# Rotary product of q and k: partner rows added by transfers of GpSimd's queue instead of by VectorE

## The chip, the core and the metric

The kernel runs on one core of one Trainium2 chip. The metric is the device time of one execution in microseconds. The core has a matrix engine (TensorE, PE in the profile, with its weight loads as PEld), a vector engine (VectorE, DVE), a scalar engine (ScalarE, ACT), GpSimd (POOL) and a queue-issuing engine (SyncE, SP). Each engine works through its own list of instructions in order; semaphores make one wait for another. Transfers (DMA) are issued by SP, ACT or POOL and then run beside the engines; those from POOL are the page's queue q0, those from SP its queue q1.

## The reference, cut to what matters

A decoder block on 512 tokens of width 1024, all in 32-bit floats:

```
h = rmsnorm(x);  [q | k | v | u_pool | u_gate] = h @ w_in
q, k: 8 heads x 2 components x 64 dims; the first 16 dims of each component are rotated:
    t1, t2 = t[..., :8], t[..., 8:16]
    t[..., :16] = [t1*cos - t2*sin, t2*cos + t1*sin]          # the other 48 dims stay
per head and block of 128 queries: p = softmax(q @ k^T, causal) for both components
    w = p[0] - lam * p[1];  o = w @ v;  rmsnorm over the 128 value dims
pooled branch from u_pool (windows 2, 4, 8, 16);  merged = sigmoid(gA)*o + sigmoid(gP)*pool
x = x + merged @ w_out
x = x + relu(rmsnorm(x) @ w_up)^2 @ w_down;  final rmsnorm
```

The scores q @ k^T do not change when the 64 dims of q and of k are put in another order, as long as both have the same one.

## The kernel before, in words

**Precision.** Each product of two float32 matrices is made of three passes of TensorE: both operands are split into a rounded high part and a low remainder (`wh_*`, `wl_*` for weights, `xh`, `xl` for activations, `gab`, `gss` for the MLP's input, `z` for its hidden layer). For weights, ACT casts the high part (L112, L120) and either DVE subtracts (L113), or ACT writes the negated high part (L121) and POOL's queue adds the weight to it by an accumulating transfer from memory (L122, 512 KB each).

**Stages.** First v for all tokens and q of head 0; from about 60 us the attention stage; from about 290 us the output projection with `w_out` (`po0_t` and `po1_t`: the two halves of the columns for the four blocks t of 128 tokens, L581 to L583); from about 350 us the MLP, to the end.

**Attention stage.** For head h, `qk(h)` projects 128 columns of q, then of k (24 matmuls of 128x512 each, L131, L132, L135; the result has 128 rows, two components of 64 dims, and 512 columns, the tokens). `rope` (L347 to L354) rotates it. The products with the tables: `q1 = acc*cosR` (L349); `sw` is a copy of acc with rows 0 to 7 and 8 to 15 of each 32 exchanged (stream_shuffle, L351); `sw = sw*sinR` (L352); `q1 = q1+sw` (L353). All four run on DVE, 128x512 each. The tables hold 1 and 0 in the rows that are not rotated; sinR holds the minus sign. The rotated q goes to `qs` (ACT casts, L375; DVE remainders, L376), the rotated k to `kz` (ACT, L379) and `ks` (ACT, L381; DVE, L382). `attn(h)` makes the scores `s` (L394, L395), the softmax (DVE L396, ACT L400), transposes the weights (`t`, L409), and multiplies with v (`o`, L417). Its result is squared and summed over rows (`sqo`, `sql` on POOL, L426, L427, on DVE for head 7; `ss` on PE, L429, L430). Between heads the list `fillers` puts 20 projections for the pooled branch and the gates (u, ga, gp); they are independent of the heads. `merge(h)` joins branches and makes `mh`, `ml`, which `w_out` needs.

**From attention to the MLP.** When `po0_t` and `po1_t` are complete, DVE adds them to x (L587), ACT squares and sums (L561), a row factor is made (ACT L571 to L573, DVE L574, L575), DVE makes `h2` of block t (L623), and PE transposes it into `h2Tt_0` and `h2Tt_1` (L629). For t = 0, 1, ACT casts these into the high part of `gab` (L641) and DVE subtracts the low part (L642); for t = 2, 3 they go through `hw`. The first products of the MLP, `um10` and `um20`, multiply the high part with the weight's high part at L759 and the low part at L761. They take 256 tokens at a time, so they need blocks 0 and 1 of `gab`.

**What sets the order.** The program is written with tiles; the framework turns it into one list for each engine at build time (`schedule_with_timeline_sim=True`, L989): it takes the operations by their place in the program and by its own estimate of when their inputs are there. Nothing is reordered when the program runs. So an edit of one step can move others on every engine. Waits come from buffers too: `q1` and `sw` have two buffers each.

Of the kernel before, what the change touches and what calls it, by code (L numbers as in the profile page):

```python
# [15 lines left out]
ALU = mybir.AluOpType  # L16
AX = mybir.AxisListType

P = 128
S = 512  # L20
D = 1024
# [21 lines left out]
    return out  # L43


SWAP = list(range(8, 16)) + list(range(0, 8)) + list(range(16, 32))

LAG = (2, 5, 7, 10, 12, 14, 15, 20)

# [2 lines left out]
def block_kernel(ctx, tc, xT, x_tok, gains, pos, consts, w_in, w_v, w_pool, w_out, w_up, w_dn, out):  # L52
    nc = tc.nc
    V, A, G, T = nc.vector, nc.scalar, nc.gpsimd, nc.tensor
# [17 lines left out]
    def bank(i, name):  # L72
        return ps.tile([P, S], F32, tag=f"b{i}", name=name)
# [13 lines left out]
    def tmp(tag, name, shape=(P, S), dt=F32, bufs=2):  # L87
        return tp.tile(list(shape), dt, tag=tag, name=name, bufs=bufs)
# [53 lines left out]
    for i in range(2):  # L142
# [19 lines left out]
    mask = cf.tile([P, S], F32, name="mask")  # L162
    G.memset(mask, 0.0)
    G.affine_select(
        out=mask[:, 384:512], in_=mask[:, 384:512], pattern=[[-1, P]],
# [51 lines left out]
    for n in range(2):  # L217
        accs = [bank((0, 1, 2, 3, 4, 5, 6, 0)[4 * n + t], f"v{n}_{t}") for t in range(NT)]
        for kk in range(4):
# [24 lines left out]
            if n == 0 and 0 < kk < 3:  # L244
                i = kk - 1
# [14 lines left out]
        for t in range(NT):  # L260
# [4 lines left out]
                out=vd[2], in0=av, scalar=rcol[:, t, 0:1], in1=vd[1],  # L265
                op0=ALU.mult, op1=ALU.subtract,
# [25 lines left out]
        out=r_, in0=posf.rearrange("p (t o) -> p t o", o=1).to_broadcast(sh),  # L292
        in1=invc.rearrange("p (o f) -> p o f", o=1).to_broadcast(sh), op=ALU.mult,
# [20 lines left out]
    arg = cf.tile([P, 2, NT, 8], F32, name="arg")  # L314
# [10 lines left out]
    for i, fill in ((0, 1.0), (1, 0.0)):  # L325
        tk = tmp("q1", f"rt{i}", (P, NT, 2, 8, 8))
        G.memset(tk, fill)
        for c in range(2):
            for x_ in range(2):
                sc = -1.0 if (i == 1 and x_ == 0) else 1.0  # L330
                V.tensor_scalar(out=tk[:, :, c, x_, :], in0=arg[:, i], scalar1=sc, scalar2=None, op0=ALU.mult)
        pt = bank((3, 2)[i], f"pt{i}")
        for t in range(NT):
            T.transpose(out=pt[:, t * P : t * P + P], in_=tk[:, t].rearrange("p c x f -> p (c x f)"), identity=ident)
        tab = cf.tile([P, S], F32, name=f"tab{i}")
        V.tensor_tensor(out=tab, in0=pt, in1=rb, op=ALU.mult)
        tabs.append(tab)
    cosR, sinR = tabs
# [8 lines left out]
    def rope(acc_, name):  # L347
        q1 = tmp("q1", f"q1{name}")
        V.tensor_tensor(out=q1, in0=acc_, in1=cosR, op=ALU.mult)  # L349
        sw = tmp("sw", f"sw{name}")  # L350
        V.stream_shuffle(out=sw, in_=acc_, mask=SWAP)  # L351
        V.tensor_tensor(out=sw, in0=sw, in1=sinR, op=ALU.mult)  # L352
        V.tensor_tensor(out=q1, in0=q1, in1=sw, op=ALU.add)  # L353
        return q1  # L354

    def proj(m, name, eng=None):
# [12 lines left out]
    def qk(h):  # L369
        qs = tp.tile([P, 2, S], F32R, tag="qs", name=f"qs{h}", bufs=2)  # L370
        ks = tp.tile([P, 2, S], F32R, tag="ks", name=f"ks{h}", bufs=2)
        kz = kzs[h % 2]
        q = rope(proj(h, f"q{h}", V) if h else q0, f"q{h}")
        for c, own, oth in ((0, lo_, hi_), (1, hi_, lo_)):
            A.copy(out=qs[own, c, :], in_=q[own])  # L375
            V.tensor_tensor(out=qs[oth, c, :], in0=q[own], in1=f(qs)[own, c, :], op=ALU.subtract)  # L376
        k = rope(proj(8 + h, f"k{h}", V), f"k{h}")
        for c, own, oth in ((0, lo_, hi_), (1, hi_, lo_)):
            A.copy(out=kz[own, c, :], in_=k[own])  # L379
        for c, own, oth in ((0, lo_, hi_), (1, hi_, lo_)):  # L380
            A.copy(out=ks[oth, c, :], in_=f(kz)[own, c, :])  # L381
            V.tensor_tensor(out=ks[own, c, :], in0=k[own], in1=f(kz)[own, c, :], op=ALU.subtract)  # L382
        return qs, ks, kz
# [609 lines left out]
```

## Time and profile before

| what | value |
|---|---|
| three runs | 677.84, 676.32, 676.32 us (median 676.32) |
| span of the profiled execution, first to last instruction | 675.2 us |
| the profiled execution's own time | not given on the page; its span lies 1.1 us under the median |
| granted TensorE clock, mean | 0.998 |
| PE busy | 665.3 us of the span (99%) |
| DVE busy | 529.1 us (78%) |
| ACT busy | 462.5 us (68%) |
| POOL busy | 123.0 us (18%), 137 instructions |
| moved by DMA | 109.34 MB, mean 162 GB/s |

The page gives busy time by engine, the same in 40 slices, the queues, the chain of work that ended last, the costliest groups of instructions and the transfers by line. Beside it stand answers about single stretches (windows), groups by line and form, and instructions in order of time. In a row of a group, the two numbers behind the bar are its busy time in us and the mean of one in ns, then the idle time of the engine just before and what ended it. A matmul of 128x512 is shown with some 390 ns, but matmuls overlap: what counts for the rate is the distance of their starts.

### The profile page before, as it was taken

Reading aid. Unit: us, or ns where it says so; the run is one execution under the profiler, and the core shown is the slowest. Engines: PE = TensorE matmul, PEld = TensorE weight load, DVE = VectorE, ACT = ScalarE, POOL = GpSimd, SP = SyncE. Lnnn points to the kernel's source line nnn. Section 1 sums busy time; section 2 is a strip of 40 time slices with the busy share of each in tenths; the row PEclk is TensorE's granted clock in tenths of the full one; section 3 lists DMA queues with packets and bytes.
Section 4 is the critical chain, followed back from the end, with each engine's and each line's share of the span. In section 5 each row is a group of like instructions: output and inputs, shape, how many; then the busy total and the mean of one; then the engine's idle time right before and its main releaser. Section 6 shows DMA issues by size and latency. Waiting matters only on the chain.

```text
span 675.2 us, 9995 instructions
## 1 busy us (share of the span) xinstructions
PE 665.3 (99%) x3686; PEld 579.9 (86%) x3686; DVE 529.1 (78%) x879; ACT 462.5 (68%) x741; POOL 123.0 (18%) x137
## 2 busy tenths in 40 slices
PE   9999999999999999999999999999999999999995
PEld 7788888888888888888889988899889998899884
DVE  6955877799979986975478989667994599747995
ACT  8465587978887698883477975367753696356874
POOL 6201110132133212520201020202103021210120
PEclk9999999999999999999999999999999999999999
DMA  8526574435254364574964678676969579493863
GB/s 272 189 71 182 126 152 125 102 94 126 87 139 105 101 171 94 126 193 177 309 194 79 196 172 241 153 179 155 234 190 197 200 156 260 125 213 131 213 125 124
DMA packets 32880, 109.34 MB, mean 162 GB/s; under 512 B 4032, under 2 KB 4928, under 8 KB 32832
## 3 DMA queue, kind: packets, MB, share of 16 engines
q0 software_dynamic: 10656, 38.80, 32.4%
q1 hardware_dynamic: 21744, 69.38, 29.0%
q8 instruction: 29, 0.48, 0.3%
q10 hardware_dynamic: 432, 0.52, 0.2%
q14 instruction: 19, 0.16, 0.1%
HBM read 106.59 MB, written 2.10 MB: 161 GB/s over the span
## 4 chain that ended last, share of the span: by engine, by line
PE 86%; DMA 5%; issue 5%; DVE 1%; ACT 1%; SPq 0%; DVEq 0%; POOLq 0%
PE dm L838 7%; PE dm L840 7%; PE dm L841 7%; PE um L759 7%; PE um L764 7%; PE um L761 7%; DMA wga_uNone<-w_up 5%; PE o L417 2%; PE ga L132 2%; PE ga L131 2%; PE gp L135 2%; PE k L132 2%; PE gp L132 2%; PE gp L131 2%; PE k L131 2%
## 5 line engine op out<-in xcount | busy, mean ns | idle before, releaser
L840 PE MATMUL dm<-wh_dt,z 128*128 128x512 f32 (+1 forms) x128 | 49.5, 387 | 0.0
L841 PE MATMUL dm<-wl_dt,z 128*128 128x512 f32 (+1 forms) x128 | 49.4, 386 | 0.0
L838 PE MATMUL dm<-wh_dt,z 128*128 128x512 f32 (+1 forms) x128 | 49.0, 387 | 0.0
L759 PE MATMUL um<-gss,wh_ut 128*128 128x256 f32 x192 | 48.1, 284 | 0.1
L761 PE MATMUL um<-gss,wh_ut 128*128 128x256 f32 x192 | 48.1, 283 | 0.0
L400 ACT ACTIVATE p<-p,st 128x128 f32<-128x128 f32 (+3 forms) x64 | 35.8, 560 | 14.1 <-DVE st L396 13.8
L112 ACT CAST wh_ut<-wga_uNone 128x1024 fp32r<-128x1024 f32 x24 | 24.9, 1053 | 28.8 <-PE dm L840 19.2
L856 DVE TENSOR_TENSOR x<-x,dm 128x512 f32<-128x512 f32 x48 | 32.8, 687 | 14.1 <-PE dm L841 14.0
L670 POOL DMA_DIRECT2D wga_dNone<-w_dn x16 | 14.2, 887 | 151.8 <-DVE wl_dt L113 151.8
L113 DVE TENSOR_TENSOR wl_ut<-wga_uNone,wh_ut 128x1024 fp32r<-128x1024 f32 x24 | 29.0, 1224 | 12.5 <-ACT wh_ut L112 12.5
L112 ACT CAST wh_ub<-wr_u 128x1024 fp32r<-128x1024 f32 x24 | 25.1, 1051 | 19.0 <-PE um L761 10.1
L670 POOL DMA_DIRECT2D wga_uNone<-w_up x18 | 15.6, 867 | 120.9 <-DVE wl_ut L113 86.9
L840 PE MATMUL dm<-wh_db,z 128*128 128x512 f32 x96 | 37.2, 389 | 0.0
L841 PE MATMUL dm<-wl_db,z 128*128 128x512 f32 x96 | 37.2, 389 | 0.0
L759 PEld LDWEIGHTS um<-gss,wh_ut 128*128 128x128 f32 x192 | 36.8, 192 | 0.3 <-ACT rawz L776 0.3
L761 PEld LDWEIGHTS um<-gss,wh_ut 128*128 128x128 f32 x192 | 36.9, 192 | 0.0
L838 PE MATMUL dm<-wh_db,z 128*128 128x512 f32 x96 | 35.8, 390 | 0.0
L113 DVE TENSOR_TENSOR wl_ub<-wr_u,wh_ub 128x1024 fp32r<-128x1024 f32 x24 | 29.2, 1222 | 7.9 <-ACT wh_ub L112 7.9
L112 ACT CAST wh_dt<-wga_dNone 128x1024 fp32r<-128x1024 f32 x24 | 24.8, 1050 | 14.6 <-issue 4.1
L735 DVE TENSOR_TENSOR z<-rawz,z 128x1024 fp32r<-128x1024 f32 x28 | 33.7, 1225 | 0.9 <-ACT z L732 0.9
L396 DVE CUSTOM_DVE_ANT_0 p<-s,mask 128x128 f32<-128x128 f32 (+3 forms) x64 | 30.3, 485 | 3.4 <-PE s L395 3.3
L732 ACT CAST z<-rawz 128x1024 fp32r<-128x1024 f32 x28 | 28.7, 1048 | 6.0 <-DVE rawz L741 4.9
(324 smaller groups left out, 2222.9 us busy)
## 6 DMA issues: line engine op xcount, KB each, us to landing
wr_u<-w_up SPq DMA_DIRECT2D x24, 512.0 KB, 5.3
wr_d<-w_dn SPq DMA_DIRECT2D x24, 512.0 KB, 4.2
wga_uNone<-w_up POOLq DMA_DIRECT2D x18, 512.0 KB, 6.7
wga_dNone<-w_dn POOLq DMA_DIRECT2D x16, 512.0 KB, 5.8
wr_k<-w_in SPq DMA_DIRECT2D x8, 512.0 KB, 3.3
wr_ga<-w_in SPq DMA_DIRECT2D x8, 512.0 KB, 3.3
wr_gp<-w_in SPq DMA_DIRECT2D x8, 512.0 KB, 4.2
wl_ga<-w_in POOLq DMA_DIRECT2D x8, 512.0 KB, 5.5
```

The source lines that it names most:

```text
L112: ins = A.copy(out=hi[:, sl], in_=raw[:, sl])
L113: (eng or G).tensor_tensor(out=lo[:, sl], in0=raw[:, sl], in1=f(hi)[:, sl], op=ALU.subtract)
L131: T.matmul(acc, lhsT=hi[:, c], rhs=rh[:, k, :], start=k == 0, stop=False)
L132: T.matmul(acc, lhsT=hi[:, c], rhs=rl[k], start=False, stop=False)
L400: A.activation(out=pr[:, c, :N], in_=pr[:, c, :N], func=AF.Exp, scale=-1.0, bias=st[:, c : c + 1], accum_out=st[:, 2 + c : 3 + c])
L735: V.tensor_tensor(out=z[:, 1], in0=r, in1=f(z[:, 0]), op=ALU.subtract)
L759: m = T.matmul(a_, lhsT=hi[:, c], rhs=rh[:, k, :], start=p + k == 0 and onto is None, stop=False, skip_group_check=True)
L761: T.matmul(a_, lhsT=hi[:, c], rhs=rl[:, k, :], start=False, stop=False, skip_group_check=True)
L764: m = T.matmul(a_, lhsT=lo[:, c], rhs=rh[:, k, :], start=False, stop=k == 3, skip_group_check=True)
L838: m = T.matmul(a_, lhsT=zh, rhs=hi[:, sl], start=p == 0 and start, stop=False, skip_group_check=True)
L840: T.matmul(a_, lhsT=zl, rhs=hi[:, sl], start=False, stop=False, skip_group_check=True)
L841: end = T.matmul(a_, lhsT=zh, rhs=lo[:, sl], start=False, stop=p == 3, skip_group_check=True)
```

## The change

The columns of q and k in `w_in` are put in another order on the host (once, outside the kernel): in each component of 64, the dims t1 stand at places 0, 8, ..., 56 and their partners t2 at places 4, 12, ..., 60; the other dims fill the places left. The tables are filled to match, with the minus sign at the t2 places of sinR. In `rope`, the shuffle (L351) and the sum (L353) go. DVE makes `q1 = acc*cosR` and `sw = acc*sinR`, both from acc. Then two accumulating transfers of POOL's queue add 16 rows of `sw` to 16 rows of `q1` each (rows 4, 12, ... to rows 0, 8, ... and the other way round; 16 rows of 2 KB, 32 KB). In the changed kernel the product from acc and sinR is L351 and the two transfers are L353; the line numbers of what runs on the chip are the same in both.

```diff
-SWAP = list(range(8, 16)) + list(range(0, 8)) + list(range(16, 32))
+ORDER = [p // 8 + 2 * (p % 8) if p % 4 == 0 else 16 + 6 * (p // 8) + p % 8 - 1 - p % 8 // 4 for p in range(64)]
...
-                sc = -1.0 if (i == 1 and x_ == 0) else 1.0
-                V.tensor_scalar(out=tk[:, :, c, x_, :], in0=arg[:, i], scalar1=sc, scalar2=None, op0=ALU.mult)
+                sc = -1.0 if (i == 1 and x_ == 1) else 1.0
+                V.tensor_scalar(out=tk[:, :, c, :, 4 * x_], in0=arg[:, i], scalar1=sc, scalar2=None, op0=ALU.mult)
...
         sw = tmp("sw", f"sw{name}")
-        V.stream_shuffle(out=sw, in_=acc_, mask=SWAP)
-        V.tensor_tensor(out=sw, in0=sw, in1=sinR, op=ALU.mult)
-        V.tensor_tensor(out=q1, in0=q1, in1=sw, op=ALU.add)
+        V.tensor_tensor(out=sw, in0=acc_, in1=sinR, op=ALU.mult)
+        for i in (0, 4):
+            G.dma_start(out=q1[i:P:8, :], in_=sw[4 - i : P : 8, :], accum_op=ALU.add)
         return q1
...
-    w_in0 = a(w_in)[0]
+    w_in0 = a(w_in)[0].copy()
+    w_in0[:, :2048] = w_in0[:, :2048].reshape(D, 32, 64)[:, :, ORDER].reshape(D, 2048)
```

The change also moves instructions on every engine, since the order is made anew. Three places follow. In these rows the digit behind a name is the head or the block of tokens; the number at the end of a name counts tiles.

POOL, around the rows of head 7, before:

```order
L122 DMA wl_ga6_2840<-w_in 128x1024
L426 TENSOR_TENSOR sqo5_2245<-o5_2240 128x512
L427 TENSOR_TENSOR sql5_2244<-sqo5_2245,sqh5_2242 128x512
L122 DMA wl_gp6_2873<-w_in 128x1024
L122 DMA wl_ga7_2906<-w_in 128x1024
```

and now:

```order
L122 DMA wl_ga6_2840<-w_in 128x1024
L353 DMA q1q7_2560<-swq7_2562 16x512 x2
L426 TENSOR_TENSOR sqo5_2245<-o5_2240 128x512
L427 TENSOR_TENSOR sql5_2244<-sqo5_2245,sqh5_2242 128x512
L122 DMA wl_gp6_2873<-w_in 128x1024
L353 DMA q1k7_2601<-swk7_2603 16x512 x2
L122 DMA wl_ga7_2906<-w_in 128x1024
```

The two transfers of q and the two of k stand in POOL's list among its sums and the transfers of weights.

PE, between the output projection and the MLP, before:

```order
L581 MATMUL po1_3_3327<-wh_o1_3_3173,vh_111 128x512
L629 MATMUL h2T0_0_3210<-ident_87,h2_2997 128x128 x4
L629 MATMUL h2T0_1_3215<-ident_87,h2_2997 128x128 x4
L629 MATMUL h2T1_0_3259<-ident_87,h2_2997 128x128 x4
L629 MATMUL h2T1_1_3264<-ident_87,h2_2997 128x128 x4
L582 MATMUL po1_3_3327<-wl_o1_3_3174,vh_111 128x512
L583 MATMUL po1_3_3327<-wh_o1_3_3173,vl_112 128x512
L759 MATMUL um10_0_3408<-gab1_2999,wh_ub11_0_0_3400 128x256
L759 MATMUL um10_1_3409<-gab1_2999,wh_ub11_0_1_3404 128x256
L759 MATMUL um20_0_3474<-gab2_3000,wh_ub21_0_0_3466 128x256
L629 MATMUL h2T2_0_3308<-ident_87,h2_2997 128x128 x4
L761 MATMUL um10_0_3408<-gab1_2999,wh_ub11_0_0_3400 128x256
```

and now:

```order
L583 MATMUL po1_3_3327<-wh_o1_3_3173,vl_112 128x512
L629 MATMUL h2T0_0_3210<-ident_87,h2_2997 128x128 x4
L629 MATMUL h2T0_1_3215<-ident_87,h2_2997 128x128 x4
L629 MATMUL h2T1_0_3259<-ident_87,h2_2997 128x128 x4
L629 MATMUL h2T1_1_3264<-ident_87,h2_2997 128x128 x4
L759 MATMUL um10_0_3408<-gab1_2999,wh_ub11_0_0_3400 128x256
L759 MATMUL um10_1_3409<-gab1_2999,wh_ub11_0_1_3404 128x256
L629 MATMUL h2T2_0_3308<-ident_87,h2_2997 128x128 x4
L759 MATMUL um20_0_3474<-gab2_3000,wh_ub21_0_0_3466 128x256
L759 MATMUL um20_1_3475<-gab2_3000,wh_ub21_0_1_3470 128x256
L629 MATMUL h2T2_1_3313<-ident_87,h2_2997 128x128 x4
L761 MATMUL um10_0_3408<-gab1_2999,wh_ub11_0_0_3400 128x256
```

The last two matmuls of the output projection stood behind the first four groups of transposes; now they stand ahead of them.

DVE, at the same place, before:

```order
L113 TENSOR_TENSOR wl_ub21_0_1_3471<-wr21_u0_3463,wh_ub21_0_1_3470 128x1024
L574 SCALAR_TENSOR_TENSOR st2_3004<-st2_3004 128x1
L575 SCALAR_TENSOR_TENSOR st2_3004<-st2_3004 128x1
L623 SCALAR_TENSOR_TENSOR h2_2997<-x1_2995,st2_3004,rawz_3003 128x1024
L642 TENSOR_TENSOR gab1_2999<-h2T0_0_3210,gab1_2999 128x4x128
L642 TENSOR_TENSOR gab2_3000<-h2T0_1_3215,gab2_3000 128x4x128
L642 TENSOR_TENSOR gab1_2999<-h2T1_0_3259,gab1_2999 128x4x128
L587 TENSOR_TENSOR x1_2995<-po1_3_3327,x1_2995 128x512
```

and now:

```order
L587 TENSOR_TENSOR x1_2995<-po1_3_3327,x1_2995 128x512
L623 SCALAR_TENSOR_TENSOR h2_2997<-x1_2995,st2_3004,rawz_3003 128x1024
L575 SCALAR_TENSOR_TENSOR st2_3004<-st2_3004 128x1
L642 TENSOR_TENSOR gab1_2999<-h2T0_0_3210,gab1_2999 128x4x128
L642 TENSOR_TENSOR gab2_3000<-h2T0_1_3215,gab2_3000 128x4x128
L623 SCALAR_TENSOR_TENSOR h2_2997<-x1_2995,st2_3004,rawz_3003 128x1024
L574 SCALAR_TENSOR_TENSOR st2_3004<-st2_3004 128x1
L113 TENSOR_TENSOR wl_ut4_0_0_3531<-wga_uNone_0_0_3392,wh_ut4_0_0_3530 128x1024
L113 TENSOR_TENSOR wl_ut4_0_1_3535<-wga_uNone_0_1_3393,wh_ut4_0_1_3534 128x1024
L575 SCALAR_TENSOR_TENSOR st2_3004<-st2_3004 128x1
L642 TENSOR_TENSOR gab1_2999<-h2T1_0_3259,gab1_2999 128x4x128
```

The sum of the last block (`x1` from `po1_3`), `h2` of blocks 1 and 2 and the splits of two weights (`wl_ut4`) now stand ahead of the low part of `gab1` that is made from `h2T1_0`.

## The prediction

> **What bounds the kernel now.** I read first the page's totals, then its chain of waits.
>
> ```profile
> span 675.2 us, 9995 instructions
> PE 665.3 (99%) x3686; PEld 579.9 (86%) x3686; DVE 529.1 (78%) x879; ACT 462.5 (68%) x741; POOL 123.0 (18%) x137
> PE 86%; DMA 5%; issue 5%; DVE 1%; ACT 1%; SPq 0%; DVEq 0%; POOLq 0%
> ```
>
> PE is busy for all but 10 us, and it makes up 86% of the chain, DVE 1%. A share over the whole span can hide a stage, so I read the windows next (start:end, length, then busy time of PE, PEld, DVE, ACT, POOL; granted clock; DMA share; GB/s):
>
> ```profile
> 60.00:330.00 270.00, 269.94 (x1290) 225.36 (x1289) 216.90 (x484) 204.24 (x373) 64.40 (x64) 1.00 0.53 139
> 150.00:180.00 30.00, 30.00 (x147) 25.11 (x146) 28.66 (x67) 24.87 (x51) 7.02 (x9) 1.00 0.42 106
> 348.00:352.00 4.00, 3.42 (x24) 2.61 (x23) 3.86 (x8) 3.40 (x7) 0.00 (x0) 1.00 0.69 240
> ```
>
> From 60 to 330 us PE is busy for 269.94 of 270 at a clock of 1.00, and also where DVE is busy for 28.66 of 30. So nothing that DVE does there sets the end, and taking work from it there wins nothing. The one hole near the change is between the output projection and the MLP, at 348 to 352, where DVE is nearly full. What moves the time is what happens there, or a wait that the change creates.
>
> **The change, part by part.** First what DVE loses, from the groups by line and form in the attention stage:
>
> ```profile
> L351 DVE STREAM_SHUFFLE swk<-k 128x512 f32<-128x512 f32 x8 | 5.9, 743 | 0.0
> L351 DVE STREAM_SHUFFLE swq<-q 128x512 f32<-128x512 f32 x8 | 5.9, 738 | 0.0
> L352 DVE TENSOR_TENSOR swq<-swq,tab 128x512 f32<-128x512 f32 x8 | 7.1, 893 | 0.1
> L352 DVE TENSOR_TENSOR swk<-swk,tab 128x512 f32<-128x512 f32 x8 | 6.6, 826 | 0.0
> L353 DVE TENSOR_TENSOR q1q<-q1q,swq 128x512 f32<-128x512 f32 x8 | 6.3, 786 | 0.0
> L353 DVE TENSOR_TENSOR q1k<-q1k,swk 128x512 f32<-128x512 f32 x8 | 6.2, 776 | 0.1
> L349 DVE TENSOR_TENSOR q1q<-q,tab 128x512 f32<-128x512 f32 x8 | 5.5, 682 | 0.0
> ```
>
> Shuffles 5.9+5.9 = 11.8 us and sums 6.3+6.2 = 12.5 us go. The 16 products with sinR, 7.1+6.6 = 13.7 us, now read acc as L349 does: 16 x 0.682 = 10.9, 2.8 less. DVE is relieved of 27.1 us, hidden behind PE's full windows: **0 us**. What it costs if that cover is wrong is the second rival.
>
> POOL gets 32 transfers. Its groups from 55 to 320 us and the page's transfers (size, median us from issue to landing):
>
> ```profile
> L427 POOL TENSOR_TENSOR sql<-sqo,sqh 128x512 fp32r<-128x512 f32 x7 | 10.7, 1521 | 0.8 <-POOL pb L447 0.4
> L426 POOL TENSOR_TENSOR sqo<-o 128x512 f32<-128x512 f32 x7 | 8.7, 1237 | 24.5 <-ACT o L421 24.5
> L122 POOL DMA_DIRECT2D wl_ga<-w_in x8 | 6.9, 866 | 30.3 <-ACT wl_ga L121 29.9 <-ACT wt L411 0.4
> wl_ga<-w_in POOLq DMA_DIRECT2D x8, 512.0 KB, 5.5
> wpr<-w_pool SPq DMA_DIRECT2D x4, 128.0 KB, 3.0
> con<-consts SPq DMA_DIRECT2D x1, 4.0 KB, 2.0
> ```
>
> Issue: 32 x 0.866 = 27.7 us on POOL, which is busy for 18% of the span. The weight transfers behind stand idle for 30.3 us waiting for ACT's L121, and their results have slack; the same tile (issues first and last, then the matmuls that use it):
>
> ```profile
> L122 POOL DMA_DIRECT2D wl_ga<-w_in x8: 847/864/886, 65.6 to 268.5; - x8
> L135 PE MATMUL ga<-xh,wl_ga x64: 387/389/477, 84.0 to 294.2; 128*128 128x512 f32 x64
> ```
>
> 84.0-65.6 = 18.4 us from issue to first use, 5.5 of it landing: some 12 us of cover. Without it, each microsecond beyond would be PE's. **0 us**.
>
> The price of one rotation is the time Y from DVE's second product to the landing of the second transfer. The trace has no 32 KB transfer of this kind inside the chip. From below: 2.0 (4 KB) after one issue, 2.9. From above: 5.5 (512 KB, the same queue, accumulating) after one issue, 6.4. I take the 3.0 of 128 KB, nearest in size from above: **Y = 0.9+3.0 = 3.9 us**. Against it stands what DVE no longer does between. Head 7's k in order of time:
>
> ```profile
> 258.04 0.69 DVE L349 TENSOR_TENSOR q1k<-k,tab 128x512 f32<-128x512 f32 x1 [1.62 <-PE k L135]
> 261.12 1.27 ACT L379 CAST kz<-q1k 64x512 fp32r<-64x512 f32 x2
> 263.26 1.26 ACT L381 CAST ks<-kz 64x512 fp32r<-64x512 f32 x2
> 264.96 0.31 PE L394 MATMUL s<-ks,qs 128*128 128x128 f32 x1
> ```
>
> The fixed part is 0.4 for the last matmul to end, 2 x 0.69 for the two products and 264.96-261.12 = 3.8 for the casts with ACT's other work between: 5.6. Head 0 has nothing between: 0.4+1.4+1.27+1.26 = 4.3. PE's lists show what stands between k's last L135 and the first L394 of that head, at the 0.227 us between starts of 512-column matmuls. In the new list the tightest heads have: head 0, 10.9; head 5, 13.2; head 7, 14.1; head 6, 14.8; the others 16 to 26. So Y may be 6.6, 7.6, 8.5 and 9.2 (in this order). Even Y = 6.4 stalls nobody: **0 us**, and a score that waits would show at L394.
>
> **The term that decides** is the move at the end of the output projection. Its rows now, DVE's and then PE's:
>
> ```profile
> 343.44 0.68 DVE L587 TENSOR_TENSOR x<-po,x 128x512 f32<-128x512 f32 x1
> 344.05 1.27 DVE L623 SCALAR_TENSOR_TENSOR h<-x,st,rawz 128x1024 f32<-128x1024 f32 x1
> 345.86 2.37 DVE L113 TENSOR_TENSOR wl_ub<-wr_u,wh_ub 128x1024 fp32r<-128x1024 f32 x2 [0.55 <-ACT wh_ub L112]
> 348.40 0.16 DVE L575 SCALAR_TENSOR_TENSOR st<-st 128x1 f32<-128x1 f32 x1
> 348.66 1.28 DVE L623 SCALAR_TENSOR_TENSOR h<-x,st,rawz 128x1024 f32<-128x1024 f32 x1
> 349.86 1.88 DVE L642 TENSOR_TENSOR gab<-h2T,gab 128x512 fp32r<-128x512 f32 x3
> 351.66 0.68 DVE L587 TENSOR_TENSOR x<-po,x 128x512 f32<-128x512 f32 x1
> ```
>
> ```profile
> 347.34 0.39 PE L581 MATMUL po<-wh_o,vh 128*128 128x512 f32 x1
> 347.57 1.91 PE L629 MATMUL h2T<-ident,h 128*128 128x128 f32 x16
> 349.82 0.87 PE L759 MATMUL um<-gab,wh_ub 128*128 128x256 f32 x3
> 351.28 0.66 PE L629 MATMUL h2T<-ident,h 128*128 128x128 f32 x4 [0.58 <-ACT h2f L646]
> 351.80 0.39 PE L761 MATMUL um<-gab,wh_ub 128*128 128x256 f32 x1
> ```
>
> Before, the first L761 starts when the third L642 ends (349.86+1.88 = 351.74). That L642 makes the low part of `gab1` from h2T1_0. The sum of `po1_3` stands behind it. In the new order the sum stands ahead, and with it other work that this L642 did not wait for. From L587(po1_3) DVE runs, at the distances above: L587 0.61 (343.44 to 344.05), L623 1.20 (348.66 to 349.86), L575 0.25 (348.40 to 348.66), two L642 1.26, L623 1.20, L574 0.25 as L575, two L113 2.37, L575 0.25, and the L642 0.63: **8.0 us**. Behind it waits PE's whole MLP.
>
> When does DVE begin? Call E the end of the last `po1_3` matmul's turn on PE. Now all six last matmuls stand ahead of the transposes, so E is 347.57+2x0.227 = 348.0 on the old clock. Ahead of L587(po1_3) stand, from `po1_2`'s sum at E-4.8 on: 0.61+0.25+1.20+2.37+0.25 and some 0.5 to 1.1 of waits for ACT's casts (0.55 at 345.86): DVE is there between E+0.4 and E+1.3; I take E+1.0. So L761 at 348.0+1.0+8.0 = 357.0, which is 5.2 after 351.80. In that time PE does what the new list puts ahead of L761 in addition, four transposes (a quarter of the 1.91 of 16, 0.5) and one L759 (0.12): 0.6. **Net +4.6 us** (4.0 to 4.9 by the bounds of DVE's arrival). ACT's cast of h2T1_0 (L641) has to be there too: in ACT's new list it stands behind two casts of weights,
>
> ```profile
> L112 ACT CAST wh_ub<-wr_u 128x1024 fp32r<-128x1024 f32 x6 | 6.3, 1047 | 0.3 <-DMA wr_u<-w_up 0.3
> ```
>
> which begin once the row factor of block 3 is made. If that takes as long as both, ACT is done 4 x 1.05 = 4.2 us after DVE's sum at E+1.6, at E+5.8, ahead of DVE at E+9.0: no term.
>
> The sum: span 675.2+0+0+0+4.6 = 679.8. The profiled execution's own time is not on the page; its span lies 1.1 under the median shown, so **680.9** measured; by itself 679.5 to 682.
>
> **Rivals.**
>
> *The rows land late (0.15; about 686).* POOL does not issue at once: in its new list transfers of q and k stand beside L426 and L427, 1.24+1.52 = 2.8 us. A transfer that is caught behind both, with the high landing, has Y = 6.4+2.8 = 9.2: head 0 waits 2.6, head 5 1.6, head 7 0.7, together 4.9, on top of the forecast: 685.8. It decides from Y = 6.6, and from about Y = 9 it costs more than the hole. Against it: L426 has 24.5 us of idle time before it, so POOL is rarely there. The Trainium skill, page "SBUF — State Buffer", section "SBUF: two separate sides", names another hold-up of this kind: while VectorE runs an operation that takes the port pair it shares with GpSimd, GpSimd can't write its descriptors, and a transfer of some 620 ns took some 3100. By its figures the estimate would be Y = 3.9+2x2.5 = 8.9 and some 685, against 680.9 without it. The issues of L122 in this trace speak against it: 847 to 886 ns, with DVE busy up to 28.66 of 30; whether descriptors are held up behind the issue, no run here shows.
>
> *Not slower: what DVE gives back, PE takes (0.25; about 676.7).* Matmuls beside a full DVE are a little longer than in the MLP:
>
> ```profile
> L131 PE MATMUL ga<-xh,wh_ga 128*128 128x512 f32 x64 | 25.3, 395 | 0.0
> L840 PE MATMUL dm<-wh_dt,z 128*128 128x512 f32 x124 | 48.3, 390 | 0.0
> ```
>
> If the 5 ns were real time and DVE's accesses their cause, 35 projections of 24 matmuls would give 840 x 0.005 = 4.2 us, and with the hole 680.9-4.2 = 676.7: no change. If besides the hole is smaller (ACT's casts earlier, DVE ahead of E), it becomes faster; I give that 0.05 of the 0.25. Against it: matmuls overlap: one is shown with 0.39 us but the next starts after 0.23 (347.34 to 347.57), so an end that is 5 ns later costs nothing by itself.
>
> *The change undone by its order.* That the sums would go back to DVE in another form can't be: L353 is a transfer in the new lists.
>
> **How the numbers follow.** Forecast 0.60, late rows 0.15, not slower 0.25. The range reaches from 676.4, half of the second rival, to 685.0, half of the first: 0.60+0.12+0.08 = 0.80. 0.3% of 676.32, about what a measurement of this kernel can tell from no change, is 2.0 us: same is 674.3 to 678.3. Faster 0.05, same 0.20, slower 0.75.
>
> **What would show it.** PE busy from 60 to 330 throughout, as before; DVE's busy time lower by 20 to 27 us; POOL's L353 at some 0.9 us and 3 us to landing; scores L394 that wait for nothing; and between 346 and 358 some 5 to 7 us in which PE stands idle, its releasers DVE's `h` and `gab`, with L113 `wl_ut` ahead of that L642. It is wrong if PE does not stand there, if L394 waits for the transfers, or if the distance between starts of L131 falls under 0.227.

## The result, and the profile after

| | kernel before | changed kernel |
|---|---|---|
| median of the runs | 676.59 us (4 runs, 676.32 to 677.84) | 684.45 us (4 runs, 683.15 to 685.67) |
| ratio, 95% interval | | 1.0111 (1.0098 to 1.0124) |
| span of the profiled execution | 675.2 us | 681.9 us (its time 683.67) |

The change made the kernel slower by 7.9 us, 1.1%. The profiled execution is one of the shorter ones of the changed kernel; the four spans go from 681.4 to 683.9. So 6.7 us can be read in the two traces, and the scatter needs a reason of its own. The page's head after:

```profile
span 681.9 us, 10019 instructions
PE 667.9 (98%) x3686; PEld 582.8 (85%) x3686; DVE 509.1 (75%) x831; ACT 461.9 (68%) x741; POOL 144.8 (21%) x169
PE 95%; ACT 2%; issue 1%; DMA 1%; POOL 1%; DVE 0%; POOLq 0%; ACTq 0%
```

DVE has 20.0 us less to do, as the change says, and the span is longer. What PE waited for between 60 and 400 us is the view that shows where (engine, operation and line, what released it, us in total, times, longest). The kernel before:

```profile
PE h2T L629 <- ACT h2f L646: 0.6, 1, 0.6
PE um L759 <- ACT gss L602: 0.3, 1, 0.3
```

The changed kernel:

```profile
PE um L759 <- ACT gab L641: 2.2, 1, 2.2
PE h2T L629 <- DVE h L623: 1.2, 1, 1.2
PE ga L131 <- DVE g L489: 1.1, 1, 1.1
PE u L131 <- DVE g L473: 1.1, 1, 1.1
```

The first two are the hole at the end of the output projection. The last two, behind the matmuls that start at 264.6 and 273.5 us, lie in the attention stage, where PE had no wait before. Together they are 5.6 us against 0.9. No score (L394) is in the list.

The end of the output projection, DVE in order of time:

```profile
350.81 0.68 DVE L587 TENSOR_TENSOR x<-po,x 128x512 f32<-128x512 f32 x1
351.41 1.27 DVE L623 SCALAR_TENSOR_TENSOR h<-x,st,rawz 128x1024 f32<-128x1024 f32 x1
352.67 1.28 DVE L642 TENSOR_TENSOR gab<-h2T,gab 128x512 fp32r<-128x512 f32 x2
353.87 1.27 DVE L623 SCALAR_TENSOR_TENSOR h<-x,st,rawz 128x1024 f32<-128x1024 f32 x1
355.19 2.35 DVE L113 TENSOR_TENSOR wl_ut<-wga_uNone,wh_ut 128x1024 fp32r<-128x1024 f32 x2
357.53 1.28 DVE L642 TENSOR_TENSOR gab<-h2T,gab 128x512 fp32r<-128x512 f32 x2
```

And PE:

```profile
350.48 1.03 PE L629 MATMUL h2T<-ident,h 128*128 128x128 f32 x8
352.74 1.09 PE L629 MATMUL h2T<-ident,h 128*128 128x128 f32 x8 [1.23 <-DVE h L623]
356.01 0.80 PE L759 MATMUL um<-gab,wh_ub 128*128 128x256 f32 x2 [2.18 <-ACT gab L641]
358.60 0.56 PE L761 MATMUL um<-gab,wh_ub 128*128 128x256 f32 x1
358.96 0.41 PE L759 MATMUL um<-gab,wh_ub 128*128 128x256 f32 x1
```

PE is done with `po1_3` at 350.48 (E in the prediction), DVE's chain from there to the L642 of h2T1_0 is the one that the order showed, and the first L761 follows it at 358.60. PE's longest wait, 2.18 us, ends with ACT's cast of h2T1_0 and not with DVE:

```profile
355.39 0.58 ACT L641 CAST gab<-h2T 128x512 fp32r<-128x512 f32 x1
```

The last row of PE shows something that the kernel before did not: matmuls of 256 columns start 0.21 us apart there instead of 0.12. The windows name it (the granted clock is the third figure from the end):

```profile
354.00:356.00 2.00, 0.00 (x0) 0.00 (x0) 2.00 (x3) 2.00 (x4) 0.00 (x0) 0.81 0.31 125
356.00:358.00 2.00, 1.99 (x9) 1.99 (x10) 2.00 (x4) 1.72 (x4) 1.01 (x2) 0.50 0.00 0
360.00:362.00 2.00, 2.00 (x12) 2.00 (x11) 1.32 (x4) 1.10 (x2) 0.00 (x0) 0.50 1.07 193
```

From about 355.2 on PE runs at half its clock, until 362.

The rows themselves. The transfers by line (median us from issue to landing), and what ACT waited for from 60 to 275 us:

```profile
q1q<-swq POOLq DMA_DIRECT2D x16, 32.0 KB, 4.4
q1k<-swk POOLq DMA_DIRECT2D x16, 32.0 KB, 3.4
```

```profile
ACT qs L375 <- DMA q1q<-swq: 11.6, 8, 2.9
ACT kz L379 <- DMA q1k<-swk: 4.0, 4, 1.4
```

From DVE's second product to the landing of the second transfer it takes 3.15 to 6.69 us, median 5.1 (from the 16 rotations' instructions and landings). ACT stands 15.6 us for it in its own list.

### The profile page after: what moved, and what is told of

It is laid out like the page before. It is cut to its first block, busy times and chain, and to the rows that moved or that the text cites. A ratio compares the mean times of both kernels' runs of the same rounds, so it can differ in the third digit from the quotient of the medians.

```text
span 681.9 us, 10019 instructions
## 1 busy us (share of the span) xinstructions
PE 667.9 (98%) x3686; PEld 582.8 (85%) x3686; DVE 509.1 (75%) x831; ACT 461.9 (68%) x741; POOL 144.8 (21%) x169
## 4 chain that ended last, share of the span: by engine, by line
PE 95%; ACT 2%; issue 1%; DMA 1%; POOL 1%; DVE 0%; POOLq 0%; ACTq 0%
PE um L759 8%; PE um L761 8%; PE um L764 8%; PE dm L838 7%; PE dm L840 7%; PE dm L841 7%; PE v L235 2%; PE ga L131 2%; PE o L417 2%; PE v L236 2%; PE ga L135 2%; PE ga L132 2%; PE po L581 2%; PE po L583 2%; PE v L237 2%; PE po L582 2%
## 5 line engine op out<-in xcount | busy, mean ns | idle before, releaser
L759 PE MATMUL um<-gss,wh_ut 128*128 128x256 f32 x192 | 48.1, 283 | 0.0
L761 PE MATMUL um<-gss,wh_ut 128*128 128x256 f32 x192 | 48.1, 283 | 0.0
L759 PEld LDWEIGHTS um<-gss,wh_ut 128*128 128x128 f32 x192 | 36.9, 192 | 0.0
L761 PEld LDWEIGHTS um<-gss,wh_ut 128*128 128x128 f32 x192 | 36.9, 192 | 0.0
L759 PE MATMUL um<-gab,wh_ub 128*128 128x256 f32 x128 | 33.8, 296 | 2.2 <-ACT gab L641 2.2
```

The costliest lines, as they stand in the source:

```text
L759: m = T.matmul(a_, lhsT=hi[:, c], rhs=rh[:, k, :], start=p + k == 0 and onto is None, stop=False, skip_group_check=True)
L761: T.matmul(a_, lhsT=hi[:, c], rhs=rl[:, k, :], start=False, stop=False, skip_group_check=True)
```

## The experiments

Two theories stood against each other. A: the loss lies in the places where the new order puts an instruction behind a wait, above all at the end of the output projection, and the rows as such cost nothing. B: rows that land late cost, wherever they are put. The order is changed by rules of the form "this instruction behind that one" (`after(later, earlier)`), which add no wait between engines; the framework then makes all lists anew around them. All ratios are to the kernel before, run on the same chip. The medians:

| run | based on | median us (runs) | ratio (95%) | profiled span |
|---|---|---|---|---|
| sum behind the low part | changed | 683.21 (4) | 1.0088 (1.0062 to 1.0113) | 678.1 |
| the new order in the kernel before | before | 680.71 (4) | 1.0060 (1.0045 to 1.0075) | 679.0 |
| fill | changed | 683.88 (4) | 1.0110 (1.0086 to 1.0135) | 683.1 |
| rows of k of head 7 first | changed | 679.02 (6) | 1.0046 (1.0029 to 1.0064) | 676.8 |
| three rules | changed | 678.20 (12) | 1.0024 (1.0006 to 1.0042) | 675.4 |
| columns alone | before | 677.42 (10) | 1.0000 (0.9990 to 1.0011) | 674.9 |
| two rules | changed | 675.84 (12) | 0.9979 (0.9966 to 0.9991) | 674.1 |
| early transposes | before | 675.34 (11) | 0.9970 (0.9960 to 0.9980) | 673.5 |

### The sum of po1_3 behind the low part

```diff
-        V.tensor_tensor(out=xs, in0=a_, in1=xs, op=ALU.add)
+        add = V.tensor_tensor(out=xs, in0=a_, in1=xs, op=ALU.add); (t, n) == (3, 1) and after(add, state["low", 1, 0])
```

> The changed kernel with one more rule for the order: DVE's sum of the last block (L587 of po1_3) is placed behind the low part of gab1 that is made from h2T1_0 (L642). DVE then has that L642 third behind the transposes, as in the kernel before; PE still has all matmuls of po1_3 ahead of the transposes; the transfers of rows are untouched. Theory A (the order at the end of the output projection costs 4.3 of the 6.7 us of span): PE stands idle for about 2 us there instead of 3.7, in pieces too short to lower the granted clock, which stays at 1.00 (0.50 from 356 to 362 in the changed kernel); the span falls from 681.9 by 4 to 5 us to 677 to 678; the waits of about 1.1 us each at 264.6 and 273.5 stay. Theory B (rows that land late are what costs, the order only moves where it shows): span over 680.5, with the idle time of PE coming back elsewhere behind 350 us.

The profiled execution did what A says: span 678.1, waits of 0.6, 0.2 and 0.5 us in place of 1.2 and 2.2, the clock at 1.00 throughout. A wait of 1.2 us came back behind, at 366 (L759 for ACT's L602). But its other three executions took 2.8 to 3.9 us longer, so that the median moved by 1.2 us only. That did not fit either theory, and two more profiles of this kernel were taken.

> The kernel of the run with the sum behind the low part, once more, for a second profile: three of its four executions took 2.8 to 3.9 us longer than the profiled one, at a clock of 0.994 to 0.996 against 0.997. If a wait of PE that grows past some 2 us lowers the clock in them, a long execution shows the granted clock at 0.50 for some 6 us directly behind one of the waits (264, 272, 350 or 366), and 2 to 4 us more there. If the transfers of rows land later in them, the waits at 264 and 272 are longer by that much and the clock stays.

> As the second look at this kernel: a third profile, to have one of a long execution.

Both caught a long execution: 681.6 and 681.2 us. In the first, ACT and PE around 265 us:

```profile
258.37 1.26 ACT L375 CAST qs<-q1q 64x512 fp32r<-64x512 f32 x2 [4.41 <-DMA q1q<-swq]
```

```profile
268.15 0.50 PE L131 MATMUL u<-xh,wh_u 128*128 128x512 f32 x1 [2.78 <-DVE g L473]
269.71 0.63 PE L131 MATMUL u<-xh,wh_u 128*128 128x512 f32 x1
270.13 0.63 PE L132 MATMUL u<-xla,wh_u 128*128 128x512 f32 x1
```

```profile
270.00:272.00 2.00, 2.00 (x6) 1.52 (x6) 1.94 (x4) 1.98 (x4) 0.00 (x0) 0.50 0.16 64
```

The rows of q of head 7 landed 7.95 us after DVE's product, behind the weight transfer `wl_ga`, which itself landed 2 us later than usual (7.5 us after its issue instead of 5.4). ACT waited 4.4 us for them where it had waited 2.4; all that stands behind in its list came 2 us later, DVE's L402 waited for that, L473 stood behind L402, and PE waited 2.8 us for L473 instead of 1.0. Some 1.5 us later its clock was halved for 3 us. From the first score of head 6 to the first matmul of the output projection this execution took 2.2 us more than the short one, although its wait at 273 went; its start had taken 1.1 more. In the second, waits were as in the short execution, but behind the same wait of 1.2 us at 369 the clock fell for one such stretch, where it had not fallen in the short one:

```profile
368.00:370.00 2.00, 0.58 (x3) 0.30 (x2) 1.78 (x3) 1.88 (x4) 0.00 (x0) 1.00 0.73 141
372.00:374.00 2.00, 2.00 (x11) 2.00 (x11) 2.00 (x3) 1.16 (x3) 0.99 (x2) 0.50 0.00 0
```

It cost 1.5 us from L764#16 to L761#48. So two causes of long executions are shown: rows that land late, through ACT's list, and a clock that falls behind some waits and not behind others of the same length. The start, 1.1 us longer in both, is a third part, and its cause stays open.

### The new order in the kernel before

```diff
+        add = V.tensor_tensor(out=xs, in0=a_, in1=xs, op=ALU.add); (t, n) == (3, 1) and (after(state["h2", 1], add), after(state["tr", 0, 0], state["mm"]))
...
+                    cast = split_w(rs[c], hi, lo, eng=V); nm + b + str(q) == "ut40" and after(state["low", 1, 0], state["split"])
```

> The kernel before, with DVE's shuffle and sums, but with rules that give it the order of the changed kernel at the end of the output projection: the last matmuls of po1_3 ahead of the transposes, DVE's sum of po1_3, h2 and the two splits of wl_ut4 ahead of the low part from h2T1_0. Up to there the lists of PE are those of before. Theory A: it loses there what the changed kernel loses, PE idle for 3 to 4 us in a row, the granted clock at 0.50 for some 6 us behind it, span 675.2 + 4.3 = 679.5 (678.5 to 681), though no row is moved by a transfer. Theory B: no more than 1 us over 675.2, since nothing lands late.

Span 679.0 against 675.2, ratio 1.0060. PE waits 1.5 us for `h` and 1.8 for ACT there, and the clock is at 0.50 behind it:

```profile
352.00:354.00 2.00, 0.67 (x3) 0.67 (x4) 2.00 (x5) 2.00 (x4) 0.00 (x0) 0.53 0.00 0
354.00:356.00 2.00, 2.00 (x12) 1.88 (x10) 2.00 (x5) 0.74 (x2) 1.42 (x2) 0.50 0.17 16
```

A kernel that moves no row by a transfer loses 3.8 us by this order alone (two groups of four transposes came out two matmuls earlier each than in the changed kernel). For this place A is right.

### The fill

```diff
+        state["fill"] = [T.matmul(fb[:, :P], lhsT=onesr, rhs=onesr, start=True, stop=True) for fb in [bank(7, "fill")] for _ in range(36)] if q == 0 else [None]; ma = product(A11, "m1")
```

> The changed kernel with 36 matmuls of 128x128 of a constant into an unused bank, placed between the transposes of h2 of block 1 and the first product of the MLP, where PE stands idle for 2.3 us; nothing reads them. The waits of DVE and ACT are unchanged. It tells apart what the wait costs and what the lowered clock behind it costs. If the clock falls because PE stood idle: it stays at 1.00 from 356 to 362, the 11 matmuls of that time take 0.12 us each again instead of 0.21, and the span falls by 1.5 to 2.5 us to 679.5 to 680.5. If the clock falls for another reason, or its loss is hidden: 681.5 to 682.5.

The 36 matmuls took 4.0 us, not the 2.3 of the hole, and this execution started 1.8 us later (first score at 81.30 instead of 79.53), so its span, 683.1, says little; nor did the median move. From the first L761 to the last, where both do the same work, it took 275.5 us against 277.1 in the changed kernel, with the clock at 1.00:

```profile
356.00:358.00 2.00, 2.00 (x20) 2.00 (x20) 2.00 (x4) 2.00 (x4) 0.00 (x0) 1.00 0.31 127
360.00:362.00 2.00, 2.00 (x20) 2.00 (x19) 2.00 (x4) 1.56 (x3) 0.76 (x1) 1.00 0.90 125
```

So the clock fell because PE stood idle, and that is worth 1.6 us behind the hole. As a gain it is lost again to the fill that was too long.

### The rows of k of head 7 first

```diff
+            add = G.dma_start(out=lo, in_=src, accum_op=ALU.add); name == "gp6" and after(add, state["row"])
...
+            state["row"] = G.dma_start(out=q1[i:P:8, :], in_=sw[4 - i : P : 8, :], accum_op=ALU.add)
```

> The changed kernel with one rule for POOL: the two transfers of k of head 7 stand ahead of the weight transfer wl_gp6, not behind it. In the changed kernel they are issued 1.4 us after DVE's product, behind that transfer, and land 6.7 us after it; ACT stands for 1.4 us at L379, and PE for 1.1 us at 273.5, after DVE L489 and ACT L506. The rule moves more: the order is made anew, and at the end of the output projection it comes out as in the kernel before (two matmuls of po1_3 behind the transposes, the third L642 ahead of the sum). Theory A: rows issued at once land after about 5 us, ACT's wait and PE's wait at 273.5 go (-1.1), the end of the output projection costs what it cost before (-4.3), the wait at 264.6, which comes from DVE's order, stays: span 676.3 to 677.3. Theory B: PE's waits in the attention stage stay or move to other heads, span over 679.

Span 676.8, ratio 1.0046. The rows of k now land 3.2 us after DVE's product instead of 6.7. PE's waits:

```profile
PE u L131 <- DVE g L473: 1.8, 1, 1.8
PE h2T L629 <- ACT h2f L646: 0.9, 1, 0.9
PE um L759 <- ACT gss L602: 0.2, 1, 0.2
```

The wait at 273.5 is gone and the end of the output projection is as before, both by one rule on POOL's list. The wait at 265 stayed and grew to 1.8: in the new order both L382 of head 7, which wait for ACT's `kz`, stand ahead of L473.

### Three rules

The rule on POOL, the sum behind the low part, and L473 of gp5 ahead of the L402 of head 6.

```diff
+        g_ = V.tensor_tensor(out=dst, in0=a_, in1=rb, op=ALU.mult)
+        name == "gp5" and after(state["rec", 6, 3], g_)
```

> The changed kernel with three rules for the order: the rows of k of head 7 ahead of the weight transfer wl_gp6 on POOL; DVE's L473 of gp5 (which frees the bank that PE waits for at 264.6) ahead of the reciprocal of block 3 of head 6 (L402, which waits for ACT); and the sum of po1_3 behind the low part from h2T1_0. The new order then has the transposes of h2 of blocks 0 and 1 eleven matmuls of po1_3 ahead of its end. The transfers of rows are all kept. Theory A: both waits of the attention stage go (-2.4), the end of the output projection costs no more than before (-4.3, up to 1 more): span 674 to 675.5, a time within 0.3% of the kernel before. Theory B (the rows' landing costs by itself, wherever it is put): at least 1% over before stays, span over 679.

Span 675.4, ratio 1.0024. At the end of the output projection PE waits no more, but one wait is left:

```profile
PE u L131 <- DVE g L473: 1.7, 1, 1.7
```

I had named L402 as what held L473 up, and freed it from that alone; the two L382 stand ahead of it now. Two of the twelve executions took 682.3 and 683.3 us, at a clock of 0.993, the others 676.7 to 680.0.

### The columns alone

```diff
+SWAP = [p ^ 4 if p % 4 == 0 else p for p in range(32)]
```

(with the column order and the tables of the change; DVE shuffles and adds as before)

> The kernel before with the column order and the tables of the change alone: the shuffle exchanges rows 0, 8, 16, 24 of each 32 with rows 4, 12, 20, 28, and DVE still adds. The lists of all engines are word for word those of before. All theories: 676.6, within 0.3% of before; if it is slower, part of the loss is the columns and not the transfers.

Ratio 1.0000 (0.9990 to 1.0011). The columns cost nothing.

### What a landing costs by itself

```diff
+            for i in (0, 4):
+                G.dma_start(out=dst[i:P:8, :], in_=src[4 - i : P : 8, :], accum_op=ALU.add)
```

(24 such pairs behind the end of the changed kernel, in four stretches)

> The changed kernel with four stretches added behind its end, which only measure: six pairs of transfers of 16 rows each (as L353 issues them), one pair after the other, with DVE idle; the same while DVE runs sums of 128x512 with two operands in the chip's memory; the same while DVE runs copies of 128x512; and six pairs with DVE idle, each directly behind an accumulating 512 KB transfer on the same queue. In the changed kernel the second row of a pair landed 3.1 to 6.7 us after DVE's product. If the queue's traffic sets it: 2.5 to 3 us from the first issue to the second landing with DVE idle and also with DVE busy, 5 to 6 behind 512 KB. If DVE holds the transfers up: 2.5 to 3 with DVE idle, 4 or more with sums or copies running.

The transfers of the stretches, us from issue to landing (min, median, max), with DVE idle, with sums, with copies, and behind 512 KB:

```profile
L948 POOL DMA_DIRECT2D x<-x x12: 750/750/1037, 683.0 to 695.9; - x12
DMA to landing us min/median/max: 2.0/2.1/2.4
...
L948 POOL DMA_DIRECT2D x<-x x10: 750/750/1036, 699.2 to 709.5; - x10
DMA to landing us min/median/max: 2.0/2.1/2.4
...
L948 POOL DMA_DIRECT2D x<-x x12: 750/751/1358, 757.8 to 771.1; - x12
DMA to landing us min/median/max: 2.0/2.1/2.7
...
L948 POOL DMA_DIRECT2D x<-x x12: 994/1196/1398, 828.9 to 857.1; - x12
DMA to landing us min/median/max: 4.5/4.8/5.0
```

With DVE running sums (0.69 us each) or copies (0.43 us each) without a pause, a transfer lands 2.1 us after its issue, as with DVE idle. Behind 512 KB on the same queue it is 4.8, and both rows of a pair land together with it. So in these stretches, where no other queue moves data, what is ahead on the queue sets the price, and DVE does not. Within the changed kernel the eleven pairs without a large transfer ahead took 4.3 to 5.9 us from the first issue to the second landing in nine rotations and 2.9 and 3.1 in two; what lengthens them there was not taken apart.

Up to its end this kernel has the lists of PE, DVE and ACT of the changed kernel, so its trace is a second execution of that one. In it the rows of q of head 7 land 8.0 us after DVE's product, behind a `wl_ga` that took 7.5 us, as in the first long execution above. ACT waits 4.4 us for them, and PE:

```profile
PE u L131 <- DVE g L473: 2.8, 1, 2.8
```

The clock is at 0.50 from 268.2 to 271.6 and from 356.9 to 363.8, and the last L761 starts at 637.8 instead of 635.7. So the late transfer and the clock lengthen executions of the changed kernel too.

### Two rules

```diff
+            state["ks", h, c] = V.tensor_tensor(out=ks[own, c, :], in0=k[own], in1=f(kz)[own, c, :], op=ALU.subtract)
...
+        g_ = V.tensor_tensor(out=dst, in0=a_, in1=rb, op=ALU.mult); name == "gp5" and [after(i, g_) for i in (state["rec", 6, 3], state["ks", 7, 0], state["ks", 7, 1])]
```

(with the rule on POOL)

> The changed kernel with two rules: the rows of k of head 7 ahead of wl_gp6 on POOL, and DVE's L473 of gp5 ahead of three operations that wait for ACT, the reciprocal of block 3 of head 6 (L402) and both low parts of k of head 7 (L382). In the run with three rules PE still stood for 1.8 us at 265, because the L382 stood ahead of L473. The end of the output projection comes out with the transposes twelve matmuls ahead of its end, with no rule there. Theory A (only places where a list stands behind a wait cost; the rows themselves cost nothing): no wait of PE over 0.5 us from 60 to 360 us, span 673 to 674.5, a time of 675 to 676.5, equal to or 0.2% under before; and if the long executions of the run with three rules (clock 0.993) are those in which the wait at 265 grew until the clock fell, they are gone, clock 0.996 or more in every run. Theory B (landing times vary and cost by themselves): long executions stay, median 0.3% or more over before.

All 32 transfers are kept, ACT still waits 11.5 us for the rows of q, and the kernel is faster than the one before: 0.9979 (0.9966 to 0.9991). PE's waits from 60 to 400 us:

```profile
PE u L131 <- DVE g L473: 0.5, 1, 0.5
PE um L761 <- DVE gab L642: 0.3, 1, 0.3
```

No execution had a clock under 0.996; the longest took 678.2 us. They lie further apart (674.1 to 678.2) than those of the next kernel (674.5 to 676.1), which has no transfers of rows.

### Early transposes in the kernel before

```diff
+        mm_ = T.matmul(a_, lhsT=mh[:, k, tsl], rhs=hi[:, sl], start=start, stop=False); (t, k) == (3, 5) and ('tr', 1, 7) in state and after(mm_, state['tr', 1, 7])
```

> The kernel before, with DVE's shuffle and sums, and one rule: the last nine matmuls of po1_3 stand behind the transposes of h2 of blocks 0 and 1. It gives the kernel before the better order that the run with two rules has at the end of the output projection, so that the two differ in the rotation alone. Theory A: the idle time of 1.2 us there goes, and the two runs are equal within 0.2%, since DVE's 27 us are hidden behind PE: span 673.5 to 674.5. If DVE's relief were worth something after all, the run with two rules would be faster than this one by 0.3% or more.

Ratio 0.9970 (0.9960 to 0.9980): the best of all, with DVE's shuffle and sums. DVE is busy for 216.78 us from 60 to 330 here and for 194.15 in the kernel with two rules:

```profile
60.00:330.00 270.00, 269.94 (x1290) 225.39 (x1289) 216.78 (x484) 203.99 (x374) 64.17 (x64) 1.00 0.52 139
```

With the end of the output projection nearly equal, 22.6 us less on DVE buy nothing: 675.84 with transfers, 675.34 without, intervals that overlap.

## Why the prediction was right, and where it was not

**Sign and place.** Slower was given 0.75, and the time lies within the range. The forecast's own 679.5 to 682 does not hold it: 4.6 us were forecast and 7.9 measured. The range reaches to 685.0 only by half of the rival of the late rows, and late rows cost at other places than that rival said. That the time lies within it is in part luck.

**DVE's relief, 0 us: right.** The rotation's own instructions lost 27.2 us, as worked out (27.1); DVE's busy time, in which overlapping instructions count once, lost 20.0, and nothing was won; the pair of the last two runs shows it without the order in the way. The rival in which PE takes what DVE gives back falls with it.

**POOL's issue and the weights behind it, 0 us: right.** PE never waited for a weight of POOL's queue.

**The end of the output projection, +4.6: right in the chain that sets it, nearly in size, and partly wrong in the wait.** DVE began the chain at E+0.3 (E+1.0 taken, 0.4 to 1.3 as bounds) and it took 7.4 us instead of 8.0, mostly since L574 and L575 cost less than 0.25 each there. L761 came at E+8.1 instead of E+9.0. But PE stood idle for 3.4 us and not for 5 to 7, and what released it last was ACT's L641, at E+5.5, which had been worked out as E+5.8 and called no term. From there PE ran eight transposes and four L759 at half the clock, for 2.6 us. At the distances of the kernel before (some 0.11 and 0.12 us) they would take 1.4, an estimate, and PE would then have stood until DVE's L642 ended at 358.2. By this estimate DVE's chain still bounds the first L761, and the half clock hid the wait for it. Against the kernel before it starts 6.8 us later, of which 2.5 had been lost ahead of E; less the 0.6 us of work that was moved ahead of it, that is 3.7. The halved clock behind the hole (+1.6 by the fill) is a term that the prediction did not have. Some 1.1 us came back behind it: from the first L761 to the last there should be 1.0 us more than before (1.6 less the 0.6 of moved work), and there is 0.1 less (277.1 against 277.2). A part of that is a hole at 379 us in the kernel before, 0.8 us over the usual distance of starts, that did not come again; the rest was not taken apart. So behind E the span is 4.2 us longer: 3.7 of hole and 1.6 of clock, less the 1.1. That this is close to the 4.6 is luck, since errors of opposite sign cancel.

**The rotation, 0 us: the step that failed.** The working set Y against what PE has between k's last matmul and the first score, and concluded: "Even Y = 6.4 stalls nobody". Y itself was 3.15 to 6.69 us with a median of 5.1, against 3.9 taken and bounds of 2.9 and 6.4 (the page had a transfer of 24.5 KB at 3.6 us, nearer in size than the 128 KB taken at 3.0). No score waited, so the comparison held. But the first to wait for the rows is ACT, and what stands behind L375 and L379 in ACT's list is not only the rotation: softmax of the head before, gates, weights. 2.4 us of waiting at L375 and 1.4 at L379, both in head 7, came out as 1.1 us each on PE, through DVE's L402 and L473, and through the table load and sigmoid of L506 and DVE's L489. I had asked what is queued behind the waiting instruction for PE and for POOL, and not for ACT. That is 2.2 us of the 6.7. In the two executions in which the `wl_ga` ahead of head 7's rows landed late, the wait at L473 grew to 2.8 us, which is a part of the scatter.

**Late rows, the first rival, 0.15.** It had the wait at the scores and a price of 4.9 us from Y = 6.6 on. The rows were late as it says, behind a transfer on their own queue (not behind L426 and L427), and they did cost, but elsewhere and less. Theory B as a whole falls with the run with two rules: late rows cost where an order puts PE's banks behind them.

**Descriptors held up by DVE.** The Trainium skill was weighed in that rival with its page "SBUF — State Buffer", section "SBUF: two separate sides", by which GpSimd can't write descriptors while VectorE runs an operation in a mode that takes the shared port pair; a 32-bit copy is the page's example. In the probe the landing is 2.1 us (median) with sums, with copies and with DVE idle: the lengthening to about 3.1 us that the page reports for a copy is not seen with these forms. The copies last 0.43 us each; what longer ones do, no run here shows.

**The clock.** The traces show 0.50 and 1.00; other figures come from windows that mix the two. Ahead of the kernel's end, the stretches at 0.50 last 3.41 or 6.83 us, and they begin within a long wait or up to 2 us behind its end. Within one execution all falls lie on one grid. In the changed kernel they come at 355.24 and, behind the last matmul, at 679.50, which is 95 times 3.413 us; in the runs with the order in the kernel before and with the second and third look at the sum the two are 95, 120 and 90 times 3.413 us apart. The Trainium skill, page "TensorE: Matmul & The Clock Gate", section "Part 1: The HAM clock gate (the "warmup" mystery)", says that the clock is halved or whole, by the activity in a window of about 3.4 us that runs freely and is not tied to the kernel. The halves, the length and the grid agree with the traces. It also says that a whole idle window is needed; here a part of one was enough. Four stretches on these grids: the one ahead of the fall in the changed kernel, the one at 0.50 behind it, the one ahead of the fall in the third look, and one in the run with the rows of k first, behind which the clock stayed at 1.00:

```profile
351.82:355.24 3.42, 1.09 (x8) 0.85 (x8) 3.42 (x7) 3.32 (x8) 0.00 (x0) 1.00 0.74 293
355.24:362.07 6.83, 6.05 (x28) 6.06 (x29) 6.15 (x10) 5.00 (x10) 1.71 (x2) 0.50 0.60 100
367.68:371.09 3.41, 1.91 (x14) 1.50 (x13) 2.67 (x4) 3.09 (x7) 0.00 (x0) 1.00 0.53 102
264.03:267.44 3.41, 1.65 (x9) 1.20 (x8) 2.97 (x7) 3.31 (x7) 0.00 (x0) 1.00 0.69 135
```

PE's idle time is the length less the first busy time: 2.3, 1.5 and 1.8 us in the three at full clock. In all traces from 30 us on, the clock fell behind every such window at full clock with 1.97 us or more of idle time, behind none with less than 1.5, and in between behind one of three (1.50, against 1.67 and 1.76). So the idle time within one window tells the falls better than the longest wait does. The wait of 1.2 us at 369, with the one of 0.3 behind it, left 1.50 us in its window where the clock fell; the same two waits left 1.47 in the second look, where it did not. What decides so near the limit was not settled.

## What to carry to other kernels

Where a result is taken off an engine and handed over by a transfer, follow the first engine that waits for it through its whole list, not only the chain that the result belongs to. Where a framework makes the order anew, look at the rows around the stage changes on every engine before costing the edit: here the order at one stage change cost 3.8 us of span without the edit, and two rules made up for all that the changed kernel had lost. And a wait on the matrix engine has a second price, the clock behind it, which comes in some executions only.

## What was not expected of the hardware

- The granted clock at 0.50 for some 7 us behind 3.4 us of waits in two pieces (1.2 and 2.2), worth 1.6 us; no wait of the kernel before (0.6 at most) had done so. The falls of one execution lie whole multiples of 3.413 us apart, and 1.5 to 2.0 us of idle time within one such window can be enough.
- A 16-row, 32 KB accumulating transfer within the chip lands 2.1 us after its issue on a quiet queue and 4.8 behind 512 KB; a pair takes 2.9 on the quiet queue, and in the kernel most pairs took 4.3 to 5.9 although no large transfer of their own queue was ahead.
- The same weight transfer landed 5.4 us after its issue in one execution of a kernel and 7.5 in another, and through ACT's list 1.8 of these 2 us reached PE (a wait of 2.8 us instead of 1.0).
